# One stationary tile for the two parts of a small expert's tokens, and a branch around the third product

## Chip, core and metric

One core of a Trainium2 chip runs the whole program. Its engines work beside each other, each on its own list of instructions in order, and meet at semaphores: TensorE (PE, matrix products, with the weight loads PEld), VectorE (DVE), ScalarE (ACT), GpSimd (POOL) and SyncE (SP), which issues the loads from HBM. The metric is the device time of one execution in microseconds (us), the median of several.

## What is computed

The reference is two transformer blocks of two layers over 256 tokens of 1024 features, in float32. The change touches the last layer alone, a mixture of eight experts with 3584 hidden features each, of which every token takes two:

```python
D_MODEL, SEQ, N_EXPERTS, TOP_K, EXPERT_FF = 1024, 256, 8, 2, 3584

def swiglu_2(x, w_gate, w_up, w_down):
    return (jax.nn.silu(x @ w_gate) * (x @ w_up)) @ w_down

def moe_ffn(h, router_w, router_b, w_gate, w_up, w_down):
    t = h.reshape(b * s, d)
    logits = (t @ router_w).astype(jnp.float32) + router_b.astype(jnp.float32)
    top_vals, top_idx = lax.top_k(logits, TOP_K)
    top_w = jax.nn.softmax(top_vals, axis=-1)
    gates = jnp.sum(jax.nn.one_hot(top_idx, N_EXPERTS) * top_w[..., None], axis=1)
    for e in range(N_EXPERTS):
        y = swiglu_2(t, w_gate[e], w_up[e], w_down[e])
        out = out + gates[:, e:e + 1] * y
```

## The kernel before

Products keep float32's accuracy by splitting both operands into a rounded part and the rest, each in the format that TensorE takes at one column per cycle (float32r): x = xh + xl and w = wh + wl, and x w is xh wh + xl wh + xh wl. Three products stand for one. A weight arrives as a `raw` tile of 128 x 1024 (512 KB, one load on SP's queue, L320); ScalarE copies it to `hi` (L331, the rounded part) and VectorE subtracts to get `lo` (L332). There are 3 buffers for `hi`, 3 for `lo`, and in the experts 27 for `raw` once the pools of the layer before have been taken over.

`route` finds each token's two experts, its place (slot) at each of them and its gates. `gather` builds, for one expert or for a pair, one-hot matrices OH from the slots (tokens on partitions, 128 slots along), and multiplies the tokens' two parts HH and HL with them: XG holds an expert's tokens with features on partitions, 8 tiles of 128 x 128 for each part. It also makes OT (the one-hot transposed, to bring results back) and RX (the norm's scale of each slot).

The work of an expert goes in 7 steps `(e, fb)` of 512 hidden columns. `gate_up` makes two banks `gu` of 128 slots x 512 columns, gate and up: for each of 8 feature tiles k it takes XG's tile as the stationary operand and streams the weight,

```python
self.mm(ps, ps, xh, wh[:, c], k == 0, False)
self.mm(ps, ps, xl, wh[:, c], False, False)
self.mm(ps, ps, xh, wl[:, c], False, k == DT - 1)
```

48 products a step. Then come the activation `sl` (ScalarE's Silu, L1740; VectorE's product with up, L1741), and, one step later, `down`: four transposes of `sl` (L277), its two parts `hh` and `hl` (L357, L358), and 24 products into two banks `y`. After an expert's seventh step `scatter` brings `y` back to the tokens. Gathers are called after the fifth step of experts 0, 1, 3 and 5, for one, two, two and two experts; the first expert's stands ahead of all.

An expert may hold up to 128 tokens. If one has more, a second pass over all experts follows (`run(P)` under `tc.If(most > P)`, L1819); it is left out here. The order on each engine is set by a scheduler when the program is built: it may move instructions within a stretch of code without branches, and then it is fixed.

All matmuls are recorded by the helper `mm` (L259), so the profile's rows tell them apart by their tiles.

Of the kernel before, what the change touches and what calls it, by code (L numbers as in the profile page):

```python
# [9 lines left out]
F32 = mybir.dt.float32  # L10
F32R = mybir.dt.float32r
# [16 lines left out]
# ---------------------------------------------------------------- column layout of the packed vectors  # L28
# [35 lines left out]
def _const_arrays():  # L64
# [58 lines left out]
    # trailing means less the token itself: tokens s of a first tile to t of both, and of a second to its own  # L123
# [16 lines left out]
# ---------------------------------------------------------------- host layout  # L140
# [22 lines left out]
def _pack(inp):  # L163
# [9 lines left out]
    for l in range(2):  # L173
# [12 lines left out]
        # an even head's turned rows come after its others, an odd one's before  # L186
# [21 lines left out]
    # key and query, value, and gate tiles, in the order of the heads' work  # L208
# [34 lines left out]
# ---------------------------------------------------------------- kernel  # L243
class _K:
# [12 lines left out]
    # ---- tensor engine  # L257
# [21 lines left out]
    # ---- constants  # L279
# [27 lines left out]
    # ---- weights  # L307
# [45 lines left out]
    # ---- splits and norms  # L353
# [14 lines left out]
    def rows(self, cols, width, dst, tile_):  # L368
        """dst[f, t] = cols[t][:, head of f]: columns over tokens spread along the partitions."""
# [4 lines left out]
    def norm(self, acc, n, eps):  # L374
        """acc: [P, S] squares summed over feature tiles -> (columns [P, 2], rows [P, S])."""
# [25 lines left out]
    def prep(self, gname, gi):  # L401
        """Splits of x * g for all feature tiles, and the row scale to apply after the product."""
# [9 lines left out]
    # ---- dense feed forward  # L412
# [35 lines left out]
    # ---- rope tables  # L448
    def rope_tables(self, pool):
        nc = self.nc  # L450
        with self.tc.tile_pool(name="rope", bufs=1) as rp:
# [17 lines left out]
            for j in range(4):  # L469
                # phase of a quarter turn for the cosines  # L470
# [1467 lines left out]
```

## Time and profile before

| what | value |
|---|---|
| median of 3 runs | 2650.4 us (2649.74 to 2652.24) |
| span of the profiled execution | 2645.7 us |
| TensorE busy | 2605.0 us, 98% of the span |
| VectorE busy | 2001.3 us, 76% |
| ScalarE busy | 1610.3 us, 61% |
| loads of expert weights | 668 of 512 KB and 8 of 256 KB |
| mean granted TensorE clock | 0.995 |

The span runs from the first to the last instruction; the time of a run has some microseconds around it. The experts take about the last 1000 us. A share over the whole span mixes stages with different limits, so the views that matter are cut to the experts. The duration of a matmul overlaps the next one's, so what one costs is read from the distance between starts.

### The profile page before, as it was taken

What the parts mean: (1) busy time and instruction counts of PE and PEld (TensorE: products, weight loads), DVE (VectorE), ACT (ScalarE), POOL (GpSimd) and SP (SyncE); (2) the same over time, 40 slices, a digit from 0 to 9 for tenths busy, and PEclk for the clock granted to TensorE, in tenths of its full rate; (3) what the DMA queues carried; (4) which work ended last, traced back from release to release, by engine and by line L of the source; (5) the groups of instructions that cost most, each with busy time, mean ns of one, the idle gap of its engine ahead of it and who ended that gap; (6) DMA issues with size and microseconds to landing.
All of it is one profiled execution on the core that took longest, in us unless ns stands there. A gap on an engine that the chain in (4) does not pass through costs nothing.

```text
span 2645.7 us, 44986 instructions
## 1 busy us (share of the span) xinstructions
PE 2605.0 (98%) x17519; PEld 2365.1 (89%) x17519; DVE 2001.3 (76%) x2624; ACT 1610.3 (61%) x2208; POOL 86.7 (3%) x85
## 2 busy tenths in 40 slices
PE   8999999999999999999999999999999999999997
PEld 8999899999999899999999988888888888888886
DVE  7658567656658577656666867898989898989897
ACT  5444455444444555455445766777777777777776
POOL 0003000000003000000000200000000000000000
PEclk9999999999999999999999999999999999999999
DMA  6554125555554125555555339899999999999992
GB/s 232 190 183 160 56 79 163 187 184 184 185 184 159 62 81 172 187 185 167 188 187 166 120 132 338 312 336 355 336 367 354 341 351 364 352 340 354 363 353 96
DMA packets 166621, 602.08 MB, mean 228 GB/s; under 512 B 18704, under 2 KB 19232, under 8 KB 166400
## 3 DMA queue, kind: packets, MB, share of 16 engines
q1 hardware_dynamic: 165792, 596.92, 64.5%
q8 instruction: 139, 2.28, 0.3%
q0 software_dynamic: 608, 2.21, 0.3%
q14 instruction: 82, 0.67, 0.1%
HBM read 596.96 MB, written 1.05 MB: 226 GB/s over the span
## 4 chain that ended last, share of the span: by engine, by line
PE 93%; issue 3%; DVE 2%; ACT 1%; DMA 0%; POOL 0%; DVEq 0%; SPq 0%; ACTq 0%; POOLq 0%
PE m L259 24%; PE mm L259 23%; PE gu L259 22%; PE y L259 11%; PE s L259 6%; PE t L259 3%; PE x L259 1%; PE x L277 1%; PE s L500 1%; DVE lo L332 1%; PE u L259 1%; ACT hi L331 0%; PE c L259 0%; PE s L277 0%; ACT xh L360 0%
## 5 line engine op out<-in xcount | busy, mean ns | idle before, releaser
L331 ACT ACTIVATE hi<-raw 128x1024 fp32r<-128x1024 f32 x1128 | 1176.1, 1055 | 824.2 <-issue 323.3
L332 DVE TENSOR_TENSOR lo<-raw,hi 128x1024 fp32r<-128x1024 f32 x1128 | 1356.0, 1222 | 422.7 <-ACT hi L331 417.7
L259 PE MATMUL gu<-hi,XG 128*128 128x512 f32 x1792 | 559.9, 397 | 0.1
L259 PE MATMUL m<-xh,hi 128*128 128x256 f32 x1760 | 495.2, 281 | 9.2 <-ACT xh L360 8.7
L259 PE MATMUL m<-xh,lo 128*128 128x256 f32 x1760 | 495.4, 282 | 3.0 <-DVE lo L332 3.0
L259 PE MATMUL m<-xl,hi 128*128 128x256 f32 x1760 | 494.9, 281 | 1.8 <-DVE xl L361 1.8
L259 PEld LDWEIGHTS gu<-hi,XG 128*128 128x128 f32 x1792 | 337.1, 189 | 80.3 <-ACT hi L331 0.6
L259 PE MATMUL gu<-lo,XG 128*128 128x512 f32 x896 | 348.0, 398 | 0.0
L259 PEld LDWEIGHTS m<-xh,hi 128*128 128x128 f32 x1760 | 333.0, 189 | 9.8 <-ACT xh L360 9.1
L259 PEld LDWEIGHTS m<-xh,lo 128*128 128x128 f32 x1760 | 332.9, 189 | 3.9 <-DVE lo L332 3.9
L259 PEld LDWEIGHTS m<-xl,hi 128*128 128x128 f32 x1760 | 332.7, 189 | 2.4 <-DVE xl L361 2.4
L259 PE MATMUL mm<-hl,hi 128*128 128x256 f32 x880 | 248.2, 282 | 0.0
L259 PE MATMUL mm<-hh,lo 128*128 128x256 f32 x880 | 248.2, 282 | 0.0
L259 PE MATMUL mm<-hh,hi 128*128 128x256 f32 x880 | 247.6, 282 | 0.0
L259 PE MATMUL mm<-xh,hi 128*128 128x256 f32 x832 | 240.8, 290 | 6.1 <-DVE x L1128 3.2
L259 PE MATMUL mm<-xl,hi 128*128 128x256 f32 x832 | 239.9, 289 | 0.0
L259 PE MATMUL mm<-xh,lo 128*128 128x256 f32 x832 | 238.2, 287 | 0.1
L259 PEld LDWEIGHTS gu<-lo,XG 128*128 128x128 f32 x896 | 169.0, 189 | 41.4 <-DVE lo L332 0.9
L259 PE MATMUL y<-lo,hh 128*128 128x512 f32 x448 | 181.0, 404 | 0.0
L259 PE MATMUL y<-hi,hh 128*128 128x512 f32 x448 | 177.7, 397 | 0.7 <-ACT hh L357 0.7
L259 PE MATMUL y<-hi,hl 128*128 128x512 f32 x448 | 178.0, 397 | 0.0
L259 PEld LDWEIGHTS mm<-hl,hi 128*128 128x128 f32 x880 | 168.2, 191 | 0.0
(551 smaller groups left out, 3448.3 us busy)
## 6 DMA issues: line engine op xcount, KB each, us to landing
raw<-in_moe SPq DMA_DIRECT2D x668, 512.0 KB, 5.3
raw<-in_ffn SPq DMA_DIRECT2D x330, 512.0 KB, 4.2
raw<-in_win SPq DMA_DIRECT2D x56, 512.0 KB, 3.6
raw<-in_dnin SPq DMA_DIRECT2D x32, 512.0 KB, 3.5
raw<-in_wout SPq DMA_DIRECT2D x16, 512.0 KB, 3.5
raw<-in_pin SPq DMA_DIRECT2D x8, 512.0 KB, 4.3
raw<-in_dnout SPq DMA_DIRECT2D x8, 512.0 KB, 3.6
raw<-in_moe SPq DMA_DIRECT2D x8, 256.0 KB, 5.5
```

What stands on the lines that cost most here:

```text
L259: ins = self.nc.tensor.matmul(out, lhsT=lhsT, rhs=rhs, start=start, stop=stop)
L277: self.nc.tensor.transpose(out, in_, self.c("ident"))
L331: nc.scalar.activation(hi[:, c], raw[:, c], AF.Copy)
L332: nc.vector.tensor_tensor(lo[:, c], raw[:, c], hi[:, c].bitcast(F32), OP.subtract)
L500: nc.tensor.transpose(p4[:, h, :].bitcast(F32R), YP[:, h, 1, :], self.identr)
```

## The change

For an expert of at most 64 tokens (`few`), slots 64 to 127 are free. The rounded part of its tokens goes to slots 0 to 63 and the rest to slots 64 to 127 of the same stationary tile. With it, one product with wh gives xh wh in the upper half of the rows and xl wh in the lower, and the product with wl adds xh wl and xl wl. The third product is not needed. Since the Silu is not linear, gate's two halves have to be added before it: a matmul with the matrix FO (identity, plus the identity with its halves exchanged where the expert is small) folds the bank `gu[0]`, by way of a copy `both`. Up's halves need no fold, since everything behind them is linear and the scatter's one-hot now holds both slots of a token.

- `route`: the counts per expert are compared with 64.5, `few` and `many` are kept, `many` goes to the integer tile `ci` as well, and `keyl` is the slot for the rest (64 further on where the expert is small).
- `gather`: a second one-hot OL from `keyl`, OB as the maximum of both (in the room of `hh`) for OT and RX, and XG's first part as rounded part plus `few` times the rest, its second part times `many`.
- `gate_up`: the products with xl come last, in a branch that TensorE alone compares; the last product with wl stands behind it. All four `hi` of gate or of up are so held until then.
- `moe`: TensorE reads the eight `many` into registers before the first gather.
- buffers: `hi` has 3 + 4 (in turn), `raw` 21 where there were 27. The second pass (`base`) keeps its third product.

```diff
-NRB, NRC, NRD, NRE, NRF = 8, 12, 4, 3, 2
+NRB, NRC, NRD, NRF, NH2 = 8, 9, 4, 2, 4
...
-        hi = self.T(self.hip, [P, 1024], "hi", F32R)
+        self.nhi += 1
+        hi = self.T(self.hips[self.nhi % len(self.hips)], [P, 1024], "hi", F32R)
...
+        few, many = self.T(keep, [P, NE], "few"), self.T(keep, [P, NE], "many")
+        nc.vector.tensor_scalar(few, pc[:, 0:8], 64.5, None, OP.is_lt)
+        nc.vector.tensor_scalar(many, few, -1.0, 1.0, OP.mult, OP.add)
+        nc.vector.tensor_copy(ci[:, 1:], many)
+        keyl = self.T(keep, [P, 2, NE], "keyl")
+        nc.vector.scalar_tensor_tensor(keyl, few[:, None, :].broadcast_to([P, 2, NE]), 64.0, sel, OP.mult, OP.mult)
+        nc.vector.tensor_tensor(keyl, keyl, key, OP.add)
...
+                    nc.vector.tensor_scalar(OL[:, t, u, :], self.c("iota"), keyl[:, t, e:e + 1], None, OP.is_equal)
+
+            OB = self.T(p1, [P, 2, 2, P], "hh")[:, :, 0:w, :]
+            nc.vector.tensor_tensor(OB, OH.bitcast(F32), OL.bitcast(F32), OP.max)
...
-                if w == 2:
-                    nc.vector.tensor_copy(XG[0][:, :, k, :], p4[:, :, 0, :])
-                    nc.scalar.activation(XG[1][:, :, k, :], p4[:, :, 1, :], AF.Copy)
...
+                low = self.T(p1, [P, 2, P], "low")
+                nc.scalar.activation(low, p4[:, 1], AF.Copy)
+                for j in range(2):
+                    u, kk = (j, k) if w == 2 else (0, k + j)
+                    e = es[u]
+                    nc.vector.scalar_tensor_tensor(XG[u][:, 0, kk, :], low[:, j, :], few[:, e:e + 1], p4[:, 0, j, :],
+                                                   OP.mult, OP.add)
+                    nc.scalar.activation(XG[u][:, 1, kk, :], p4[:, 1, j, :], AF.Copy, scale=many[:, e:e + 1])
...
+            FO = self.T(pool, [P, 2, P], "FO")
+            if not base:
+                for u, e in enumerate(es):
+                    nc.vector.scalar_tensor_tensor(FO[:, u, :], SELF, few[:, e:e + 1], self.c("ident"), OP.mult, OP.add)
...
+                        for k in range(len(ws) - 2, len(ws)):
+                            self.mm(ps, ps, XG[:, 0, k, :], ws[k][0], k == 0, False)
+                            if k < DT - 1:
+                                self.mm(ps, ps, XG[:, 0, k, :], ws[k][1], False, False)
+
+                def third():
+                    for k in range(DT):
+                        self.mm(ps, ps, XG[:, 1, k, :], ws[k][0], False, False)
+
+                if base:
+                    third()
+                else:
+                    with tc.If(self.many[e] > 0):
+                        third()
+                self.mm(ps, ps, XG[:, 0, DT - 1, :], ws[-1][1], False, True)
...
+        def activate(gu, RX, FO):
+            if not base:
+
+                both = self.T(pool, [P, 512], "both")
+                nc.scalar.activation(both, gu[0], AF.Copy)
+                self.mm(gu[0], gu[0], FO, both, True, True)
...
+        pe = mybir.EngineType.PE
+        self.many = [nc.values_load(ci[0:1, 1 + e:2 + e], engines=(pe,), min_val=0, max_val=1) for e in range(NE)]
...
+            self.nhi, self.hips = -1, self.hips * 3 + [pool("hi2", NH2)] * NH2
```

The names in the order's rows are tiles: `gu` the two banks of a step, `hi` and `lo` the weight's parts, XG the gathered tokens, `x` a bank for gathers, transposes and scatters. TensorE, where gate of a step of the first expert ends and up begins, before:

```order
L259 MATMUL gu_20692<-hi_20721,XG_19699 128x512 x2
L259 MATMUL gu_20692<-lo_20722,XG_19699 128x512
L259 MATMUL gu_20692<-hi_20725,XG_19699 128x512 x2
L259 MATMUL gu_20741<-hi_20746,XG_19699 128x512 x2
L259 MATMUL gu_20692<-lo_20726,XG_19699 128x512
```

The same place in the changed kernel, where `gu_20286` is gate and `gu_20336` up:

```order
L259 MATMUL gu_20286<-hi_20315,XG_19795 128x512
L1772 COMPARE_AND_BRANCH
L259 MATMUL gu_20286<-hi_20291,XG_19795 128x512 x2
L259 MATMUL gu_20286<-hi_20295,XG_19795 128x512 x2
L259 MATMUL gu_20286<-hi_20311,XG_19795 128x512 x2
L259 MATMUL gu_20286<-hi_20315,XG_19795 128x512 x2
L1772 UNCONDITIONAL_BRANCH x2
L259 MATMUL gu_20286<-lo_20316,XG_19795 128x512
L259 MATMUL gu_20336<-lo_20342,XG_19795 128x512
```

The eight products with the second part moved behind all others but one, into the branch; each `hi` is read once ahead of it and twice within. Waits and semaphore instructions are left out of these rows.

TensorE at the start of the experts, between `route`'s last product and the first gather, before:

```order
L259 LDWEIGHTS onesb_19349
L259 MATMUL s_19625<-sel_19617,onesb_19349 128x8
L259 MATMUL x_19700<-OH_19696,HH_19344 128x128
L259 MATMUL x_19710<-OH_19696,HH_19344 128x128
L259 MATMUL x_19700<-OH_19696,HL_19345 128x128 x2
```

And in the changed kernel:

```order
L259 LDWEIGHTS onesb_19349
L259 MATMUL s_19625<-sel_19617,onesb_19349 128x8
L1858 TENSOR_LOAD ci_19651
L1858 ISA x2
L259 MATMUL x_19796<-OH_19787,HH_19344 128x128 x2
L259 MATMUL x_19796<-OL_19788,HL_19345 128x128 x2
```

Eight such reads of `ci` with their two register instructions each stand there now, one after another, ahead of the first gather.

TensorE at the end of a gather for one expert (its transposes and its product with RS), before:

```order
L259 MATMUL gu_20529<-lo_20539,XG_19699 128x512
L277 MATMUL x_20682<-c_id_82,OH_20638 128x128 x2
L259 MATMUL gu_20529<-hi_20558,XG_19699 128x512 x2
L259 MATMUL x_20687<-RS_19580,OH_20638 128x1 x2
L259 MATMUL gu_20529<-lo_20559,XG_19699 128x512
```

And in the changed kernel, where the one-hots' maximum lies in a tile `hh` and `sl` are the activations of two steps:

```order
L259 MATMUL gu_20917<-lo_20947,XG_19795 128x512
L259 MATMUL gu_21030<-hi_21035,XG_20788 128x512
L277 MATMUL x_20849<-c_id_82,hh_20786 128x128 x2
L259 MATMUL x_20854<-RS_19580,hh_20786 128x1 x2
L277 MATMUL x_20967<-c_id_82,sl_20864 128x128 x4
L277 MATMUL x_21130<-c_id_82,sl_21027 128x128 x4
L259 MATMUL y_3431_20058<-hi_20980,hh_20972 128x512
```

The transposes of two steps' activations now stand in a row behind the gather's, and the products `y` of the first of them follow at once.

## Rows read from the trace of the kernel before

**Rows 1.** Stretches: us, busy (x) PE, PEld, DVE, ACT, POOL; clock, DMA share, GB/s.

```profile
1650.00:2600.00 950.00, 950.00 (x4258) 768.38 (x4257) 852.46 (x827) 721.58 (x787) 0.00 (x0) 1.00 0.95 346
2062.16:2079.46 17.30, 17.30 (x77) 13.95 (x77) 15.35 (x15) 13.23 (x15) 0.00 (x0) 1.00 1.00 373
2200.00:2250.00 50.00, 50.00 (x221) 40.30 (x221) 44.57 (x41) 37.77 (x40) 0.00 (x0) 1.00 0.99 364
1595.00:1625.00 30.00, 27.14 (x219) 26.52 (x218) 20.67 (x54) 17.49 (x33) 0.71 (x1) 0.92 1.02 408
1620.00:1625.00 5.00, 5.00 (x23) 4.71 (x23) 1.89 (x7) 0.60 (x1) 0.00 (x0) 0.54 1.03 417
```

**Rows 2.** Waits from 1650 to 2600 us: total, times, longest, in us.

```profile
ACT hi L331 <- PE gu L259: 121.3, 221, 2.0
DVE lo L332 <- ACT hi L331: 92.5, 192, 1.4
...
DVE lo L332 <- DMA raw<-in_moe: 3.1, 7, 0.7
```

**Rows 3.** Chain of waits from 2000 to 2100 us: start, us, what.

```profile
2062.16 0.48 PE y L259 x2
...
2066.38 0.44 PE x L277 x4
...
2069.62 9.84 PE gu L259 x42
2079.46 0.47 PE y L259 x2
```

**Rows 4.** Groups of instructions, 1650 to 2600 us: count, busy us, mean ns, idle before.

```profile
L259 PE MATMUL gu<-hi,XG 128*128 128x512 f32 x1698 | 529.3, 397 | 0.0
L358 DVE TENSOR_TENSOR hl<-x,hh 128x512 fp32r<-128x512 f32 x53 | 36.2, 683 | 0.0
L357 ACT ACTIVATE hh<-x 128x512 fp32r<-128x512 f32 x53 | 30.8, 582 | 0.2
L1703 DVE CAST XG<-x 128x256 fp32r<-128x256 f32 x24 | 10.0, 418 | 0.8 <-PE x L259 0.6
L1691 DVE TENSOR_SCALAR OH<-c_dn,key 128x128 fp32r<-128x128 f32 x12 | 2.7, 278 | 0.0
```

**Rows 5.** Timeline of TensorE, a float32 product in the first block: start, us.

```profile
363.45 2.86 PE L259 MATMUL t<-Uc,raw 128*128 128x256 f32 x12
365.95 0.82 PE L259 MATMUL s<-wE,SK 128*128 128x256 f32 x4
```

**Rows 6.** Timeline of TensorE near the end, a product behind a wait.

```profile
2632.73 0.50 PE L259 MATMUL x<-yh,OT 128*128 128x512 f32 x1 [0.15 <-DVE ACC L1781]
2633.06 0.40 PE L259 MATMUL x<-yl,OT 128*128 128x512 f32 x1
```

**Rows 7.** The branch over the second pass: ns min/median/max, first and last start.

```profile
L1819 PEldq COMPARE_BRANCH  x1: 3355/3355/3355, 2634.0 to 2634.0; - x1
L1819 POOLq COMPARE_BRANCH  x1: 45/45/45, 2636.7 to 2636.7; - x1
L1819 POOLq EVENT_SEMAPHORE  x1: 17/17/17, 2636.9 to 2636.9; - x1
L1819 PEldq EVENT_SEMAPHORE  x1: 51/51/51, 2637.4 to 2637.4; - x1
L1819 DVEq COMPARE_BRANCH  x1: 72/72/72, 2637.6 to 2637.6; - x1
```

**Rows 8.** SP's read of one count, and the first gather's start.

```profile
L1811 SPq TENSOR_LOAD <-ci x1: 476/476/476, 1619.5 to 1619.5; - x1
L1811 SPq SEQ_ASSERT  x1: 33/33/33, 1620.3 to 1620.3; - x1
1619.24 0.52 PE L259 MATMUL x<-OH,HH 128*128 128x128 f32 x3 [0.65 <-DVE OH L1691]
```

**Rows 9.** Waits of SP's queue from 1650 to 2600 us: total, times, longest, in us.

```profile
SPq L320 <- DVE lo L332: 664.3, 609, 7.4
```

More of the change, by code (lines that the diff above doesn't have):

```diff
@@ L1662, in route, with experts @@
         nc.vector.tensor_reduce(cm, pc[:, 0:8], AX.X, OP.max)
-        ci = self.T(keep, [P, 1], "ci", I32)
-        nc.vector.tensor_copy(ci, cm)
-        return HH, HL, ACC, RS, GT, key, ci
-    def experts(self, base, HH, HL, ACC, RS, GT, key, st):
+        ci = self.T(keep, [P, 1 + NE], "ci", I32)
+        nc.vector.tensor_copy(ci[:, 0:1], cm)
+        few, many = self.T(keep, [P, NE], "few"), self.T(keep, [P, NE], "many")
[5 more added lines that the diff above has]
+        nc.vector.tensor_tensor(keyl, keyl, key, OP.add)
+        SELF = self.T(keep, [P, P], "SELF")
+        nc.vector.tensor_copy(SELF[:, 0:64], self.c("ident")[:, 64:128])
+        nc.vector.tensor_copy(SELF[:, 64:128], self.c("ident")[:, 0:64])
+        return HH, HL, ACC, RS, GT, (key, keyl, few, many, SELF), ci
+    def experts(self, base, HH, HL, ACC, RS, GT, keys, st):
         nc, tc = self.nc, self.tc
+        key, keyl, few, many, SELF = keys
         def open_(name, bufs):
@@ L1683, in experts @@
             nc.vector.tensor_scalar(kb, key, float(base), None, OP.subtract)
-            key = kb
+            key = keyl = kb
         def gather(es):
             w = len(es)
-            OH = self.T(p1, [P, 2, 2, P], "OH", F32R)[:, :, 0:w, :]
+            OH, OL = [self.T(p1, [P, 2, 2, P], n, F32R)[:, :, 0:w, :] for n in ("OH", "OL")]
             for t in range(2):
@@ L1718, in gather @@
                 for t in range(2):
-                    self.mm(ps, ps[:, u:u + 1], OH[:, t, u, :].bitcast(F32), RS[:, t:t + 1], t == 0, t == 1)
+                    self.mm(ps, ps[:, u:u + 1], OB[:, t, u, :], RS[:, t:t + 1], t == 0, t == 1)
             RX = self.T(pool, [P, 2], "RX")
             nc.vector.tensor_copy(RX[:, 0:w], ps[:, 0:w])
-            return [(XG[u], OT[:, u], RX[:, u:u + 1]) for u in range(w)]
+            FO = self.T(pool, [P, 2, P], "FO")
+            if not base:
+                for u, e in enumerate(es):
+                    nc.vector.scalar_tensor_tensor(FO[:, u, :], SELF, few[:, e:e + 1], self.c("ident"), OP.mult, OP.add)
+            return [(XG[u], OT[:, u], RX[:, u:u + 1], FO[:, u, :]) for u in range(w)]
         def gate_up(e, fb, XG, RX):
@@ L1795, in experts @@
                     late.append(open_("moey", 1))
-                sl = gate_up(e, fb, G[e][0], G[e][2])
+                gu = gate_up(e, fb, G[e][0], G[e][2])
             if pend is not None:
@@ L1805, in experts @@
                     G += gather([pe + 1, pe + 2])
-            cur = G[e] if e is not None else None
-            pend = (e, fb, sl, cur) if e is not None else None
+            if e is not None:
+                pend = e, fb, activate(gu, *G[e][2:4]), G[e]
     def moe(self, HH, HL, ACC, RS, GT, key, ci):
@@ L1855, in build @@
             self.nraw, self.rawp, self.once, self.ahead = -1, [ring], [], []
-            self.hip = pool("hi", 3, side="right")
+            self.nhi, self.hips = -1, [pool("hi", 3, side="right")]
             self.lop = pool("lo", 3, side="right")
@@ L1913, in build @@
                 stx.close()
[L1914 to L1916 removed]
+            self.nhi, self.hips = -1, self.hips * 3 + [pool("hi2", NH2)] * NH2
+            self.nraw, self.rawp = -1, [ringb] * NRB + [ringc] * NRC + [ring] * 4
+            self.once, self.ahead = rest + [ring] * 4, ahead
             self.psx = pool("psx", 2, space=PSUM)
```

31 lines of the change are left out of this document (12 added, 19 removed).

## The prediction, as it was put on record

> **What bounds the kernel now.** I read the busy time by stretch first [rows 1]. The eight experts run from about 1620 to 2632 us. From 1650 to 2600 us TensorE is busy for all 950 us at a granted clock of 1.00, VectorE for 852 us, ScalarE for 722 us, and the DMA engines have a share of 0.95. The waits of that stretch say who follows whom [rows 2]: no matmul stands in the list, ScalarE's `hi` waits for TensorE to free a buffer (121.3 us behind `gu` alone), VectorE's `lo` for `hi` (92.5 us), and either for a weight's DMA only 3.1 us. The chain of waits is then TensorE alone [rows 3]: 42 gate and up products in 9.84 us, 0.2343 us each, and from 2062.16 to 2079.46 one step (one block of 512 hidden columns of one expert): 17.30 us. Counted out, 72 products x 0.2343 + 0.44 us for the four transposes = 17.31 us. So TensorE waits for nothing, and a product left out there is worth 0.234 us until another engine is late. That other engine is close: the same step holds 15.35 us of VectorE [rows 1].
>
> The stretch has 1698 gate and up products with `hi` [rows 4], 32 to a step, so 53.1 steps: 17.90 us each for TensorE (0.6 us of it gather and scatter), 852.46 / 53.1 = 16.05 us for VectorE, 13.6 us for ScalarE. There are 56 steps.
>
> **How often the product goes.** The reference's router, worked out on its own default inputs, gives the experts 64, 59, 68, 59, 84, 64, 57 and 57 tokens. So six have at most 64 (42 steps) and two have more (14 steps).
>
> **TensorE, an expert of few tokens.** Gone: 16 products x 0.2343 = 3.75 us. New: the fold, a 128x512 product of two plain float32 operands. No such row exists; the nearest is 128x256 in float32, which the profile shows as two instructions, 12 of them from 363.45 to 365.95 us [rows 5]: 0.208 us each, 0.417 us for 256 columns, 0.83 for 512. I take 0.85. New too: two skipped branches. In the built program the skipped side is a wait until TensorE's own count stands at everything issued so far, a jump, and on. So the queue runs empty each time. The matmul ends 0.397 us after its start, where the next would have started at 0.234: 0.16 us. After a wait the first product takes 0.50 us, and the next starts 0.33 us after it [rows 6]: 0.10 us more. An event instruction of TensorE took 51 ns and a compare 45 to 72 ns on four engines [rows 7]; with the jump some 0.15 us. Sum 0.41; I take 0.45 us a skip. The ends are far apart: not below 0.16 us, which the drain alone takes [rows 4, 6], and up to 3.36 us, which TensorE's one compare took where it left out the whole second pass of the experts [rows 7]. I take the low end because this jump passes 8 products and their weight loads, not thousands of instructions; POOL, whose skipped part is one instruction, went on 0.2 us after its compare.
>
> The Trainium skill (Runtime: NRT & Kernel Launch, Instruction fetch mechanics) says that a taken branch whose target lies outside the part of the program held at the engine waits for a fetch. By that rule the 3.36 us are such a fetch, which agrees with the row, and it speaks against this change: a skip pays it where its target lies past the end of what is held, and what that would make of the time stands with the rivals.
>
> Step: 17.90 - 3.75 + 0.85 + 0.90 = 15.9 us.
>
> **VectorE takes over.** Its 16.05 us stay and the gather grows, per pair of experts: four more one-hot fills (0.278 us), one maximum over 128x512 (nearest 0.683 us), two masks (0.28), and 16 three-operand writes of 128x128 for eight casts of 128x256 at 0.418 us [rows 4]; a new one lies between the 0.278 of that shape and the 0.418, I take 0.3. Sum 1.1 + 0.7 + 0.6 + 1.5 = 3.9 us per pair, 0.28 us per step: 16.3 us. So with 15.9 for TensorE and 16.3 for VectorE the step is VectorE's. It never ran at 100%, since it waits for `hi`, and `hi` for buffers that TensorE frees. The change raises `hi` from three buffers to seven but holds four until the branch. I walked a step through by hand: after a gate's branch the next four `hi` are made in 4 us while three `lo` (3.5 us) are still to be made from `hi` that exist, so VectorE has work. I add 0.3 us for what does not fit: 16.6 us.
>
> ScalarE gains the copy `both` (0.58 us, as `hh`) and 0.34 us of gather: 14.5 of 16.6 us, hidden. DMA: 12 loads of 512 KB in 16.6 us are 379 GB/s against 364 in the best 50 us of this stretch and 408 with a deep queue [rows 1]: it just fits, with 21 buffers where there were 27. Each other engine also gets a jump per branch, 112 of them at some 0.05 us, beside operations of 1.2 us: hidden; bare, 6 us.
>
> **An expert of many tokens** keeps every product and stays TensorE's: 17.90 + 0.85 + 2 x 0.1 for compare and jump = 18.95 us.
>
> **The start.** TensorE now reads eight counts before the first gather. On SP such a read took from 1619.5 to 1620.3 us with what belongs to it [rows 8], 0.85 us; eight are 6.8 us, on the path, since the gather began at 1619.24 us [rows 8], as soon as its one-hot was there. I take 7. After the wait for the router the granted clock was 0.54 for 5 us [rows 1], near the lower of its two levels; a longer wait meets the same fall, so I add nothing for it.
>
> **Gathers.** The new maximum tile takes the room of `hh`, so the next step's `hh` waits for its readers: the order shows two steps' transposes in a row behind them. `hh` and `hl` then stand bare (0.58 + 0.68 us): 1.3 us x 4 gathers, 5 us.
>
> **Sum.** 42 x (16.6 - 17.9) = -55; 14 x (18.95 - 17.9) = +15; start +7; gathers +5: -28 us. The profiled execution spans 2645.7 us against a median of 2650.4, 4.7 us lie around it, and the change is the same in both: 2618 in the span, **2622 us**.
>
> **Rivals.** *The skip is dear.* TensorE's step is 15.0 + 2s us with a skip of s. At s = 1.2 it is 17.4, 42 x 0.5 = 21 us of gain, and the 27 us of cost eat it: from there the kernel is slower. At 2 us the step is 19.0: +46 + 27, 2723 us; at the 3.36 us of the row it is 21.7 and the time 2837; if one skip in ten pays that, 8 x 3.36 = 27 us more, 2649, no change. For it: the one compare that TensorE ran. Against: its distance, and that four engines' compares took 0.07 us or less. The Trainium skill's rule on fetches (above) would make it some of the skips, not all. *DMA is the next bound.* At 364 GB/s, the best 50 us [rows 1], a step takes 6.29 MB / 364 = 17.3 us: -25 + 27, 2652 us, no change. For it: a share of 0.99 there; against it: 0.95 in the mean, 408 GB/s with a deep queue, and SP's waits, which are for VectorE to free a buffer, 664 us [rows 9]. *The two engines fit without loss* and skips hide: 15.9 us, -84 + 27, 2593 us. *The change doesn't do what it says:* if the two experts at exactly 64 count as many, 28 x -1.3 + 28 x 1.05 + 12 = +5, 2655 us.
>
> **How the numbers follow.** 0.2% is 5 us, about what a measurement of this kernel can tell. Forecast with its own range of 2605 to 2640 us: 0.57, all faster. Dear skips, all or some: 0.20, of it 0.16 slower, 0.04 the same. DMA: 0.13, split 0.04 faster, 0.05 same, 0.04 slower. No loss: 0.06. Not as it says: 0.04, half same, half slower. Faster 0.67, same 0.11, slower 0.22. The range goes down to 2596 (part of the no-loss case stays out) and up to 2690, a skip of 1.6 us; some 0.16 of the chance lies outside.
>
> **What would show it.** Waits of TensorE for `lo` in the experts of few tokens, VectorE above 95% busy there, steps of 16.6 us in experts 0, 1, 3, 5, 6, 7 and near 19 us in 2 and 4; gaps of 0.45 us in TensorE before the last `lo` product of gate and of up; the first gather some 7 us later. It is wrong if the gaps are over 1 us, if `lo` or `hi` wait for DMA, or if VectorE is idle while TensorE waits, which would mean that the held `hi` buffers starve it.

## Result: 70 us slower

The changed kernel takes 2720.4 us (median of 4 runs, 2720.2 to 2721.6) where the kernel before took 2650.1 us beside it (4 runs, 2649.0 to 2652.2): a ratio of 1.027, with a 95% interval of 1.0255 to 1.0284. The forecast was 2622 us in a range of 2596 to 2690: wrong in its sign and outside its range. The profiled execution spans 2718.3 us, 72.6 more than before.

From the profile page of the changed kernel: busy time, share of the span and instructions of each engine.

```profile
PE 2581.9 (95%) x16959; PEld 2265.3 (83%) x16959; DVE 2011.6 (74%) x2696; ACT 1628.6 (60%) x2332; POOL 87.3 (3%) x85
```

Its busy times by stretch, with the columns of [rows 1]: the experts, a stretch in which the tokens of experts 2 and 3 are gathered, and one step of a small expert.

```profile
1650.00:2680.00 1030.00, 943.34 (x3796) 684.86 (x3795) 871.37 (x892) 749.81 (x912) 0.00 (x0) 0.97 0.89 325
...
1882.00:1902.00 20.00, 11.49 (x42) 8.58 (x40) 8.87 (x27) 11.22 (x24) 0.00 (x0) 0.63 0.32 127
2096.79:2113.79 17.00, 15.61 (x64) 10.95 (x63) 15.15 (x15) 13.14 (x16) 0.00 (x0) 1.00 0.98 361
```

Before, TensorE was busy for every microsecond of the experts [rows 1]. Now it is busy for 943 of 1030 us, VectorE for 871, the DMA share has fallen from 0.95 to 0.89: no engine is full, so they wait for each other. In the 20 us of the gather no engine is busy for 60%, and the granted clock there is 0.63.

The waits of the changed kernel from 1650 to 2680 us (total, times, longest) answer to [rows 2]:

```profile
ACT hi L332 <- issue: 93.1, 47, 3.1
...
DVE lo L333 <- PE gu L259: 54.9, 49, 2.4
ACT hi L332 <- PEq L1772: 53.8, 25, 2.7
PEld y L259 <- ACT hi L332: 42.4, 57, 1.1
...
PEld gu L259 <- ACT hi L332: 31.9, 40, 3.0
```

ScalarE's `hi` now waits for L1772, the branch (53.8 us by name; of the 93.1 us put down to "issue", for which the view names no releaser, 58.7 us end within 0.4 us of a skip's last instruction). And TensorE's weight loads now wait for `hi`, which is not in the list before. It is a circle.

To see where the time went, take the distances between the starts of VectorE's `sl` (L1741 before, L1786 after): there is one in each of the 56 steps, so 55 distances, the time ahead of the first and the time behind the last. The distances fall into 12 in which a gather runs (the last three of experts 0, 1, 3 and 5), 14 that start in the experts of many tokens, 2 and 4, and 29 others of small experts. Worked out so from each profiled execution, less the same of the kernel before (1639.8 us ahead of the first, 504.3 in the 29 steps, 227.1 in the 12, 245.9 in the 14, 28.7 behind the last; it took 2648.7 to 2650.1 us beside these runs):

| kernel | median us | ratio to before (95%) | start | 29 small steps | 12 gather steps | 14 large steps |
|---|---|---|---|---|---|---|
| after | 2720.4 | 1.0270 (1.0255 to 1.0284) | +13.0 | -1.9 | +43.0 | +18.4 |
| e1_no_branch | 2639.2 | 0.9956 (0.9942 to 0.997) | +10.3 | -39.7 | +15.3 | +6.6 |
| e2_hold_one | 2652.7 | 1.0012 (1.0002 to 1.0022) | +14.8 | -34.2 | +19.7 | +7.7 |
| e3_hi_11 | 2682.7 | 1.0122 (1.0106 to 1.0139) | +19.9 | -21.8 | +26.0 | +11.6 |
| e4_rooms | 2690.6 | 1.0154 (1.0137 to 1.0171) | +15.7 | -7.9 | +22.0 | +13.2 |
| e5_gather_sum | 2676.6 | 1.0103 (1.0086 to 1.0119) | +11.0 | -8.6 | +7.0 | +18.7 |
| e6_no_branch_gather_sum | 2610.4 | 0.9851 (0.9835 to 0.9867) | +3.3 | -33.9 | -12.4 | +6.5 |
| e7_hold_two | 2697.3 | 1.0181 (1.0164 to 1.0198) | +14.3 | -13.8 | +33.9 | +15.0 |
| e8_hold_two_gather_sum | 2669.1 | 1.0075 (1.0056 to 1.0093) | +10.6 | -12.7 | +10.1 | +12.0 |
| e9_no_branch_gather_sum_hh2 | 2606.4 | 0.984 (0.9824 to 0.9857) | +6.5 | -39.2 | -12.3 | +4.4 |
| e10_hold_two_gather_sum_hh2 | 2662.9 | 1.0052 (1.0035 to 1.0069) | +16.8 | -14.7 | +8.5 | +11.8 |
| e11_hi_10_gather_sum_hh2 | 2655.5 | 1.0025 (1.0014 to 1.0036) | +11.9 | -16.8 | -1.1 | +14.5 |
| e12_both_on_vector | 2671.1 | 1.0081 (1.0064 to 1.0098) | +18.0 | -11.9 | +11.5 | +10.2 |
| e13_up_only_hi_7 | 2640.8 | 0.9973 (0.9963 to 0.9982) | +6.2 | -11.4 | -7.1 | +5.8 |
| e14_up_only_hi_9 | 2636.8 | 0.9954 (0.9937 to 0.997) | +9.3 | -14.7 | -9.6 | +8.3 |

The four columns are of one execution each; the one of e10 took 5 us more than e10's median.

By the prediction's own sum the row of the changed kernel should have read +7, 29 x -1.3 = -38, 12 x -1.3 + 5 = -11, +15. So the start missed by 6 us, the large experts by 3, the small steps by 36 and the gathers by 54: together 99 us, for the 98 between 2622 and 2720. The two big ones are the question.

The 36 us of the small steps don't lie evenly. The first two distances of experts 1, 3, 5 and 6, behind the end of the expert before, take 17.0 and 23.8 us, where they took 19.7 and 16.8: 17 us more for the eight, where 10 less had been forecast. The other 21, of 17.0 us mostly, take 19 us less, where 27 had been forecast.

### The profile page after: what moved, and what is told of

Same layout as the page of the kernel before. It is cut to its first block, busy times and chain, and to the rows that moved or that the text cites. A ratio compares the mean times of both kernels' runs of the same rounds, so it can differ in the third digit from the quotient of the medians.

```text
span 2718.3 us, 44878 instructions
## 1 busy us (share of the span) xinstructions
PE 2581.9 (95%) x16959; PEld 2265.3 (83%) x16959; DVE 2011.6 (74%) x2696; ACT 1628.6 (60%) x2332; POOL 87.3 (3%) x85
## 5 line engine op out<-in xcount | busy, mean ns | idle before, releaser
L332 ACT ACTIVATE hi<-raw 128x1024 fp32r<-128x1024 f32 x1128 | 1142.3, 1052 | 823.5 <-issue 420.6
L259 PE MATMUL gu<-hi,XG 128*128 128x512 f32 x1120 | 404.7, 400 | 18.5 <-ACT hi L332 16.6
L259 PE MATMUL gu<-lo,XG 128*128 128x512 f32 x896 | 381.9, 433 | 19.5 <-DVE lo L333 6.1
L259 PEld LDWEIGHTS gu<-hi,XG 128*128 128x128 f32 x1120 | 211.2, 189 | 88.0 <-ACT hi L332 33.8
L259 PE MATMUL y<-hi,hh 128*128 128x512 f32 x448 | 188.4, 425 | 29.9 <-ACT hi L332 17.2
L259 PE MATMUL y<-lo,hh 128*128 128x512 f32 x448 | 173.7, 401 | 0.0
L259 PEld LDWEIGHTS mm<-hh,lo 128*128 128x128 f32 x880 | 168.3, 191 | 0.0
```

The source lines that it names most:

```text
L259: ins = self.nc.tensor.matmul(out, lhsT=lhsT, rhs=rhs, start=start, stop=stop)
L332: nc.scalar.activation(hi[:, c], raw[:, c], AF.Copy)
```

## A small step: held `hi`

ScalarE and VectorE in the step of 17.00 us shown above: start, us, instruction, and in brackets the idle time before it with what ended it.

```profile
2101.40 0.58 ACT L358 ACTIVATE hh<-x 128x512 fp32r<-128x512 f32 x1
2103.15 3.91 ACT L332 ACTIVATE hi<-raw 128x1024 fp32r<-128x1024 f32 x4 [1.18 <-issue]
2106.97 0.57 ACT L1782 ACTIVATE both<-gu 128x512 f32<-128x512 f32 x1
2110.22 2.96 ACT L332 ACTIVATE hi<-raw 128x1024 fp32r<-128x1024 f32 x3 [2.68 <-PEq L1772]
...
2103.73 4.62 DVE L333 TENSOR_TENSOR lo<-raw,hi 128x1024 fp32r<-128x1024 f32 x4
2108.63 1.23 DVE L333 TENSOR_TENSOR lo<-raw,hi 128x1024 fp32r<-128x1024 f32 x1 [0.28 <-issue]
2110.81 2.36 DVE L333 TENSOR_TENSOR lo<-raw,hi 128x1024 fp32r<-128x1024 f32 x2 [0.95 <-PE gu L259]
2113.79 0.75 DVE L1786 SCALAR_TENSOR_TENSOR sl<-gu,RX,sl 128x512 f32<-128x512 f32 x1 [0.62 <-ACT sl L1785]
```

TensorE's waits for `hi` in the same step:

```profile
2105.22 0.50 PE L259 MATMUL y<-hi,hh 128*128 128x512 f32 x1 [0.69 <-ACT hi L332]
...
2107.12 0.50 PE L259 MATMUL y<-hi,hh 128*128 128x512 f32 x1 [0.23 <-ACT hi L332]
```

ScalarE stops for 2.68 us until the branch behind up has freed the bank's first `hi`, and 1.18 us earlier on. Each stop ends just behind a branch. TensorE then waits for the `hi` made behind gate's branch (0.69 and 0.23 us), and so comes later to up's. VectorE idles for 0.28 + 0.95 + 0.62 us: with its 15.15 us of work that makes the 17.00. The first two of these waits are not for `hi`: they end with TensorE's products with `lo`, the 0.95 us with the product behind up's branch, which frees a buffer of `lo`. The third is for ScalarE's `sl`, which stands behind the `hi` that came late. So all three engines turn on TensorE's way to the branch. The skip itself is no matter. TensorE's last product ahead of that branch and the first behind it, from the timeline:

```profile
2109.70 0.40 PE L259 MATMUL gu<-hi,XG 128*128 128x512 f32 x1
2110.24 0.47 PE L259 MATMUL gu<-lo,XG 128*128 128x512 f32 x1
```

The branch's own instructions, from the view of L1772: count, then least, median and most ns, first and last start:

```profile
L1772 PEldq COMPARE_BRANCH  x140: 65/202/368, 1641.0 to 2688.0; - x140
L1772 PEldq EVENT_SEMAPHORE  x84: 51/51/51, 1642.4 to 2688.8; - x84
```

The 84 skips are 42 steps x 2, as predicted. From the last product ahead of a skip to the first behind it are 0.54 us, 0.31 more than between two products, and in all 84 places between 0.30 and 0.32. The Trainium skill's rule (Runtime: NRT & Kernel Launch, Instruction fetch mechanics) that a taken branch whose target lies outside what the engine holds waits for a fetch shows in none of them.

A step of the other kind, behind the end of expert 2 (2072.99 to 2096.79 us), has 40 `y` products in it where the step above has 24, since a part of the step before's falls into it. ScalarE's stops for the branches stand in it too, this one and one of 2.73 us:

```profile
2086.10 3.90 ACT L332 ACTIVATE hi<-raw 128x1024 fp32r<-128x1024 f32 x4 [2.23 <-PEq L1772]
```

**e1, the branch away.** Small experts make no third product, large ones make it in its old place; no reads of counts.

```diff
+                            if base or e in (2, 4):
+                                self.mm(ps, ps, XG[:, 1, k, :], ws[k][0], False, False)
...
-                    with tc.If(self.many[e] > 0):
-                        third()
...
-        self.many = [nc.values_load(ci[0:1, 1 + e:2 + e], engines=(pe,), min_val=0, max_val=1) for e in range(NE)]
```

> The changed kernel without its branches and without the eight register reads: which experts are small is written into the program for this input (0, 1, 3, 5, 6, 7 make no third product; 2 and 4 make it in its old place, beside each weight's first product). The packed tokens, the fold, the longer gather, 7 buffers for hi and 21 for raw stay as in the change. Changed kernel 2720 us, before 2650. Theory A (the branches cost: hi held until the branch, and work that can't be ordered across a branch): a step of a small expert is VectorE's 16.3 to 16.6 us instead of 17.0, the steps behind an expert's end lose their 4.3 us, gathers spread among the products again; worked out as in the prediction without skips and reads, 42 x (16.45 - 17.9) + 14 x 0.85 + 10 us for start and gathers = -39 us against before, 2611 us, 2600 to 2635. Rival B (fold, gather and VectorE cost, branches don't): start 6 of the 13 us and the gathers' 43 us stay, so 2690 to 2710 us.

2639.2 us: 81 us below the changed kernel, so theory A holds in size, though its 2600 to 2635 was too hopeful: the small steps came down by all that had been forecast (-39.7), the gathers only from +43 to +15. The eight distances behind an expert's end keep 4 of their 17 us with no branch at all; what holds those is open.

**e2, the branch stays and holds one.** It tells the two halves of theory A apart.

```diff
                             self.mm(ps, ps, XG[:, 0, k, :], ws[k][0], k == 0, False)
+                            if base or (e in (2, 4) and k < DT - 2):
+                                self.mm(ps, ps, XG[:, 1, k, :], ws[k][0], False, False)
...
-                    for k in range(DT):
+                    for k in range(DT - 2, DT):
                         self.mm(ps, ps, XG[:, 1, k, :], ws[k][0], False, False)
```

> The branches stay at their places, in all experts, but hold only the last two of the eight third products, which read the last hi; in experts 2 and 4 the other six stand in their old place (written into the program for this input), in the small ones they are left out as in the change. So the branch, its skip and the cut in the program's order stay, and of the four held hi one is. If the held buffers are what starves the engines (theory A1): clean steps of small experts go from 17.0 to about 16.4 us, some 30 x 0.6 = 18 us, and the 4.3 us at each of six experts' ends and a part of the gathers' 43 us go: 2660 to 2690 us. If it is the cut in the order and the skip (theory A2): within 6 us of the changed kernel, 2714 to 2726 us.

2652.7 us, below what A1 gave and far from A2: with the branches, skips and reads all in place, holding one `hi` in place of four is worth 68 us. Of the 66 between the two profiled executions 32 lie in the small steps (12 of them in the eight behind an expert's end), 23 in the gather steps, and 11 in the large experts, whose products e2 also moves back to their old place. Branches, skips and reads together are the rest to e1, 13 us. One step of a small expert without the branch (e1), by stretch:

```profile
1806.47:1821.47 15.00, 14.79 (x63) 10.92 (x63) 15.00 (x16) 13.36 (x16) 0.00 (x0) 1.00 1.03 409
```

And one with a branch that holds one (e2):

```profile
2448.80:2464.20 15.40, 15.03 (x62) 10.65 (x61) 14.99 (x15) 13.49 (x16) 0.00 (x0) 1.00 1.02 401
```

Without the hold VectorE is full and the step is 15.0 us. The 16.3 us that the prediction took for VectorE's work were the mean of all steps; one without gather and scatter had 15.35 us of it before the change [rows 1].

**e3, more buffers** in place of fewer held.

```diff
-NRB, NRC, NRD, NRF, NH2 = 8, 9, 4, 2, 4
+NRB, NRC, NRD, NRF, NH2 = 8, 5, 4, 2, 8
```

> The changed kernel with 11 buffers for hi in place of 7, and 17 for raw in place of 21 to make room. Theory A1 (held hi): with four held there are 7 left to run ahead in, as good as without a hold: 2660 to 2690 us, unless loads come late with 17 buffers, which would show as waits of hi or lo for a DMA above 20 us in the experts. Theory A2 (cut order, skip): 2714 to 2726 us. Theory B (rooms of the gather): 2714 to 2726 us.

2682.7 us: as A1 says, 38 us less, with no wait for a DMA among the long ones. But the small steps gain 20 us of the 32 that e2 gains: 14.4 to 16.8 us each. ScalarE's longest wait in total is now another, `hh` for the `y` products of the step before (70.0 us from 1660 to 2620 us).

**e7, two held**, by twice as many branches; nothing left out.

```diff
-                def third():
-                    for k in range(DT):
-                        self.mm(ps, ps, XG[:, 1, k, :], ws[k][0], False, False)
+                    def third():
+                        for k in range(4 * q, 4 * q + 4):
+                            self.mm(ps, ps, XG[:, 1, k, :], ws[k][0], False, False)
```

> The changed kernel with a branch after each pair of hi, four to a step in place of two, so that two hi are held in place of four; nothing is left out. With one held (e2) a clean step was 15.2 to 15.4 us, with four 17.0. Held buffers: TensorE's own step is 72 - 16 products, the fold and four skips, 13.1 + 0.44 + 0.85 + 4 x 0.35 = 15.8 us, VectorE's 15.0; clean steps of 15.8 to 16.2 us, 2660 to 2685 us. If a branch costs by itself more than a held buffer does: above 17.0 us a step, 2720 us or more.

2697.3 us, a gain of 23 us and 12 us short of what was expected: steps of 15.7 to 16.8 us. Twice the branches are not dearer than the two buffers that they free, but they give little.

## The gather: a chain through two engines

TensorE, ScalarE and VectorE of the changed kernel while the tokens of experts 2 and 3 are gathered:

```profile
1888.15 0.80 PE L259 MATMUL x<-OH,HH 128*128 128x256 f32 x2 [3.01 <-ACT XG L1732]
...
1889.99 0.80 PE L259 MATMUL x<-OH,HH 128*128 128x256 f32 x2 [0.62 <-ACT XG L1732]
...
1887.99 0.38 ACT L1726 ACTIVATE low<-x 128x256 f32<-128x256 f32 x1
1888.78 0.37 ACT L1732 ACTIVATE XG<-x,many 128x128 fp32r<-128x128 f32 x1 [0.42 <-DVE XG L1730]
1889.57 0.37 ACT L1732 ACTIVATE XG<-x,many 128x128 fp32r<-128x128 f32 x1 [0.42 <-DVE XG L1730]
1889.83 0.38 ACT L1726 ACTIVATE low<-x 128x256 f32<-128x256 f32 x1
...
1900.75 0.60 ACT L358 ACTIVATE hh<-x 128x512 fp32r<-128x512 f32 x1 [2.65 <-PE x L277]
1904.36 1.06 ACT L332 ACTIVATE hi<-raw 128x1024 fp32r<-128x1024 f32 x1 [3.02 <-PE y L259]
...
1888.40 0.35 DVE L1730 SCALAR_TENSOR_TENSOR XG<-low,few,x 128x128 fp32r<-128x128 f32 x1 [0.71 <-ACT low L1726]
1889.18 0.35 DVE L1730 SCALAR_TENSOR_TENSOR XG<-low,few,x 128x128 fp32r<-128x128 f32 x1 [0.43 <-ACT XG L1732]
```

Each new operation takes what the prediction gave it (0.35 us for 0.3). But they follow each other: `low` on ScalarE, XG on VectorE, XG on ScalarE, both once more, then TensorE's next bank, 1.84 us from one `low` to the next. Of the eight rounds of this gather the last five (`low` from 1887.99 to 1895.93 us) have no `hi` and no `lo` between them: while they run, the weights stand still, TensorE with them. Behind them ScalarE waits for the transposes of two steps and for `y` products, and makes the next `hi` at 1904.36 us. In the gather for experts 4 and 5 the last four rounds stand so, in that for 6 and 7 the last two; the three distances of these gathers take 72.7, 69.3 and 65.3 us, where each took 57.0. Fewer such rounds cost less, but the last gather loses 8 us with two. Before the change a bank had two casts, with `hi` and `lo` and products of gate and up between:

```profile
2096.50 0.42 DVE L1703 CAST XG<-x 128x256 fp32r<-128x256 f32 x1
2096.75 0.37 ACT L1704 ACTIVATE XG<-x 128x256 fp32r<-128x256 f32 x1
2097.08 1.06 ACT L331 ACTIVATE hi<-raw 128x1024 fp32r<-128x1024 f32 x1
```

**e4, rooms of its own** for the maximum OB, and two buffers for `low`.

```diff
-            OB = self.T(p1, [P, 2, 2, P], "hh")[:, :, 0:w, :]
+            OB = self.T(p1, [P, 2, 2, P], "OB")[:, :, 0:w, :]
...
-                low = self.T(p1, [P, 2, P], "low")
+                low = self.T(pool, [P, 2, P], "low")
```

> The changed kernel with a room of its own for the maximum OB (it shared hh's) and two buffers for low; 20 buffers for raw in place of 21. If the gathers' 43 us and the late start come from these rooms (theory G): the steps with a gather lose 8 to 10 us each and the start 2 us, 2675 to 2690 us. If they come from the branch, behind which a gather's work is not ordered among other products (A2), or from held hi (A1): each gather 1 to 2 us better, 2712 to 2720 us.

2690.6 us, 30 us less, near theory G: the gathers give 21 of it back, not the 32 to 40 expected, and the start nothing. The run changes both rooms at once. Its gathers for a pair take 70.2, 65.2 and 54.5 us: the last, made of the same operations, is below the 57.0 of before. There `hi` stand between them on ScalarE:

```profile
2405.95 0.38 ACT L1726 ACTIVATE low<-x 128x256 f32<-128x256 f32 x1
2406.23 1.05 ACT L332 ACTIVATE hi<-raw 128x1024 fp32r<-128x1024 f32 x1
2407.18 0.36 ACT L1732 ACTIVATE XG<-x,many 128x128 fp32r<-128x128 f32 x1
2407.43 1.06 ACT L332 ACTIVATE hi<-raw 128x1024 fp32r<-128x1024 f32 x1
```

As far as this gather shows, the rounds cost what the order of the program makes of them; the three operations more that a bank has cost little there.

**e5, another gather.** TensorE adds the two parts, so that the copies are those of before. The maximum with its room in `hh` goes as well.

```diff
+                        nc.vector.tensor_scalar(OL[:, t, u, :], self.c("iota"), keyl[:, t, e:e + 1], few[:, e:e + 1],
+                                                OP.is_equal, OP.mult)
...
+                    for i, parts in enumerate((((HH, OH), (HL, OL)) if not base else ((HH, OH),), ((HL, OH),))):
+                        for n, (src, one) in enumerate(parts):
+                            for t in range(2):
+                                self.mm(ps, p4[:, i, j * w:j * w + w, :], src[:, t, (k + j) * P:(k + j) * P + P], one[:, t],
+                                        n == 0 and t == 0, n == len(parts) - 1 and t == 1)
+                if w == 2:
+                    nc.vector.tensor_copy(XG[0][:, :, k, :], p4[:, :, 0, :])
+                    nc.scalar.activation(XG[1][:, :, k, :], p4[:, :, 1, :], AF.Copy)
```

> The changed kernel with another gather: TensorE adds the two parts itself (products of HH with OH and of HL with OL into one bank, OL filled as one-hot times few, so that it is empty for a large expert), XG is written by one 128x256 copy for each expert as before the change, and OT and RX come from OH and OL in turn, so that OB, its room and low are gone. Branches and the four held hi stay. If the gathers' 43 us come from the chain that ScalarE and VectorE take in turn (low 0.38, XG 0.35, XG 0.37, XG 0.35, XG 0.37 us, 1.85 us a feature tile where TensorE has 0.8 us of products): 3 x 12 + 4 = 40 us less, 2675 to 2690 us. If they come from the branch, behind which a gather's work can't be ordered among other products: 2710 to 2720 us.

2676.6 us: 44 us less, 36 of it in the gather steps, though the branches are all there. TensorE at the gather of experts 2 and 3 in e5, where the gather's products stand among others again:

```profile
1858.32 0.40 PE L259 MATMUL x<-OH,HH 128*128 128x256 f32 x2
...
1858.80 0.39 PE L259 MATMUL x<-OH,HL 128*128 128x256 f32 x2
1859.03 0.40 PE L259 MATMUL gu<-lo,XG 128*128 128x512 f32 x1
```

So it was this gather's own form, chain and rooms together, and not that work can't be ordered across a branch. How the 36 us divide between the two isn't shown: e4 leaves the chain in and gives 21.

**e6, e5's gather without the branch.**

> e1_no_branch (which experts are small is written into the program for this input) with the gather of e5. e1 gave 2639 us, its clean steps 15.0 us, its steps with a pair's gather 28.6 to 32.8 us. If those steps' extra 14 to 18 us are the chain of copies: 3 x 13 = 39 us less, 2595 to 2610 us. If they are something else (the order of TensorE's work around a gather): 2630 to 2640 us.

2610.4 us, 29 us below e1: the gather alone again, chain and rooms, the held buffers being out of the way. This and e9 are what the packing is worth on this input when nothing is decided at run time: 1.5 to 1.6%.

## Looking for a version that decides at run time

**e8**, e7 and e5 together.

> e7 and e5 together; nothing is left out and nothing is written into the program for this input. If held buffers and the gather's chain are the two causes and apart from each other, the gains add: e7's time less 35 to 40 us, about 2630 us (2615 to 2650), below the kernel before. If the gather's loss goes away with the held buffers, e7's time less 10 us or so, 2660 us.

2669.1 us: 28 us below e7 where 35 to 40 were expected, and still above the kernel before. The two causes add up only in part; the small steps stay at 16.1 to 16.8 us. ScalarE's longest wait, from 1660 to 2600 us, is then this one (total, times, longest):

```profile
ACT hh L358 <- PE y L259: 72.4, 25, 4.2
```

**e9, e10, e11: two buffers for `hh` and `hl`**, in e6, in e8, and in e5 with 10 for `hi`.

```diff
-            hh = self.T(p1, [P, 4, P], "hh", F32R)
-            hl = self.T(p1, [P, 4, P], "hl", F32R)
+            hh = self.T(pool, [P, 4, P], "hh", F32R)
+            hl = self.T(pool, [P, 4, P], "hl", F32R)
```

> e6 (no branch, which experts are small written into the program for this input; TensorE sums the gather) with two buffers for hh and hl in place of one, 20 for raw. In e6 the clean steps of experts 1 and 3 took 15.0 us, those of 5 to 7 16.2 us, with ScalarE's hh waiting for the y products of the step before. If that wait is the one buffer of hh: 15.0 us there too, some 14 x 1.2 = 17 us less, about 2593 us. If it is the order that the program was given there: 2605 to 2613 us.

2606.4 us, 4 us below e6 and not 17, in the range given for the other reading, the program's order: the late steps came down from 16.2 to 15.5 us, and a gather step took part of it.

> e8 (branch after each pair of hi, so two held; TensorE sums the gather; nothing left out) with two buffers for hh and hl, 20 for raw. e8's clean steps in the later experts took 16.8 us, with TensorE busy for 15.7; ScalarE waited 2.6 us in each for the y products that read hh. If hh's buffer sets the 16.8 us: 15.8 to 16.1 us, some 25 x 0.8 + 5 = 25 us less, 2640 to 2650 us. If the branches do: 2664 to 2674 us.

2662.9 us, 6 us below e8: the late steps are at the expected 16.1 us, but those of the first two experts rose to 17.9.

> The change's own two branches a step and four held hi, with 10 buffers for hi, two for hh and hl, 17 for raw and TensorE's sum in the gather; nothing left out. e3 (11 for hi) had clean steps of 16.4, later 16.8 us with hh waiting. If buffers are what the held hi take and the rest is hh: clean steps of 15.4 to 15.8 us, 2630 to 2645 us, below the kernel before. If the hold costs whatever the buffers (work behind it can't be ordered ahead): 16.4 us and 2655 to 2670 us.

2655.5 us, 7 us above the kernel before: with buffers enough, four held cost less than two held with twice the branches, and both end at steps of 16.1 us where e9 has 15.0 to 15.5.

**e12, the copy `both` on VectorE.** In e11 ScalarE waits 49.2 us for gate's bank (2200 to 2580 us) with `hi` copies queued behind.

```diff
-                nc.scalar.activation(both, gu[0], AF.Copy)
+                nc.vector.tensor_copy(both, gu[0])
```

> e11 with the fold's copy both made by VectorE in place of ScalarE. If the copy's place in ScalarE's queue sets the 16.1 us (hi copies stand behind its wait for gate): VectorE's step is 15.0 + 0.6 = 15.6 us, some 30 x 0.5 = 15 us less than e11's 2655 us, 2638 to 2645 us. If the branch does: 2655 us or, as VectorE has more to do, up to 2665 us.

2671.1 us, 16 us slower than e11, with late steps of 16.3 us: the place of `both` alone doesn't set the 16.1 us. VectorE has more to do than ScalarE (15.3 and 12.2 us of a late step), and the wait for gate only moved to the next in ScalarE's list, `sl` (47.8 us in the same stretch). So a wait for gate in that list, with `hi` behind it, isn't ruled out as the cause.

**e13 and e14, only up packed**, so no fold and one branch a step; 7 and 9 buffers for `hi`.

```diff
+                            g = 2 if m and not base else 0
+                            self.mm(ps, ps, XG[:, g, k, :], ws[k][0], k == 0, False)
+                            if not m:
+                                self.mm(ps, ps, XG[:, 1, k, :], ws[k][0], False, False)
...
+                if m:
+                    if base:
+                        third()
+                    else:
+                        with tc.If(self.many[e] > 0):
+                            third()
```

> Only up is packed: gate's stationary tiles hold the rounded part in both halves of the slots and the rest in both halves, and gate makes all three products in their old place; up's tile holds the rounded part in slots 0 to 63 and the rest in 64 to 127, and up's third product stays in a branch. So there is no fold, no both, one branch a step, and hi is held in up alone. 7 buffers for hi, two for hh and hl, 18 for raw. TensorE's step is 64 x 0.2343 + 0.44 + 0.35 = 15.8 us, VectorE's 15.0. If the fold and gate's hold were the rest of the loss: steps of 15.8 to 16.1 us, 42 x (15.95 - 17.3) + 14 x 0.2 + 15 us for start and gathers = -39, about 2611 us (2600 to 2625), below the kernel before. If one held bank costs as much as two: steps of 16.8 us and 2640 us or more.

2640.8 us, faster than both kernels (0.27% under the one before), but 16 us above the top of what was expected, and where the other reading, that one held bank costs as much as two, had put it: steps of 16.2 us in the first experts, 17.0 from the fourth on.

> e13 with 9 buffers for hi and 16 for raw. If up's four held hi still starve ScalarE and VectorE with 7 buffers: 10 to 20 us less than e13. If they don't: within 5 us of e13, and above it by more if 16 buffers for raw are too few.

2636.8 us, 4 us less than e13: buffers were no longer the matter. This version beats the kernel before by 0.46% (0.30 to 0.63) and the changed one by 3.1% (2636.8 to 2720.4 us), with counts read at run time. An early and a late step of it, by stretch:

```profile
1814.83:1830.02 15.19, 15.04 (x68) 11.94 (x66) 15.09 (x16) 12.73 (x15) 0.00 (x0) 1.00 1.03 407
2456.07:2473.12 17.05, 16.14 (x69) 12.18 (x68) 15.06 (x14) 12.66 (x15) 0.00 (x0) 1.00 1.00 379
```

ScalarE in the late one, from the timeline:

```profile
2458.85 5.80 ACT L332 ACTIVATE hi<-raw 128x1024 fp32r<-128x1024 f32 x6
2467.65 0.69 ACT L1778 ACTIVATE sl<-gu,RX 128x512 f32<-128x512 f32 x1 [3.00 <-PE gu L259]
2468.24 5.79 ACT L332 ACTIVATE hi<-raw 128x1024 fp32r<-128x1024 f32 x6
```

And VectorE behind it:

```profile
2469.32 3.50 DVE L333 TENSOR_TENSOR lo<-raw,hi 128x1024 fp32r<-128x1024 f32 x3 [1.68 <-ACT hi L332]
```

VectorE has 15.1 us of work in either. In the late one ScalarE comes to `sl` 3.00 us before its bank is done, with six `hi` behind, and VectorE waits 1.68 us for the first of them. That the place of `sl` in the fixed list makes the two us is argued from these rows; no run moved it, and it stays open.

## Why the prediction was wrong, step by step

- **What bounds the kernel now**: TensorE, with VectorE close behind. Right, but VectorE's size was wrong. The 16.05 us are a mean that holds gather and scatter, some 0.6 us a step (32.9 us of `XG`, `OH` and `ACC` by the groups from 1650 to 2600 us, over 53.1 steps), and the 15.35 us of a step without them [rows 1] are the busy time of an engine that waits before most instructions. Where it doesn't wait, the next starts before the one ahead has ended: eight `lo` in a row in the changed kernel take 9.18 us, 1.148 each, where one alone takes 1.22. A full step is then 15.0 us (e1). This error hid a part of the next one.

```profile
1643.61 9.18 DVE L333 TENSOR_TENSOR lo<-raw,hi 128x1024 fp32r<-128x1024 f32 x8 [2.60 <-ACT hi L332]
```

  The Trainium skill (Perfetto Trace Analysis, DVE / Act Engine Instruction) says that the reported time runs to the acknowledged write, while the next instruction may begin its prefetch before that; these rows agree.
- **Six experts of few tokens, 84 skips**: right. **Products**: right. **Fold**: 0.85 predicted; from 2108.61 to 2109.70 us the fold and one product take 1.09, so 0.86. **Skip**: 0.45 predicted, 0.31 measured. The dear skip, the rival that held most of the slower side, was wrong: the kernel is slower for another reason.
- **"I walked a step through by hand ... so VectorE has work. I add 0.3 us"** is the step that failed, for the small steps: 17.0 us for 16.6, and for a possible 15.2 to 15.4 (e2). The walk looked at the time behind gate's branch, and there VectorE does have work: four `lo` from 2103.73 us on. It left out the time ahead of each: with four of seven held and three made ahead, ScalarE must stop until TensorE comes to the branch, and TensorE itself waits on its way for `hi` that ScalarE could make only behind the branch before. VectorE is busy for 89% of such a step, not for the 95% that the prediction wanted to see. e2 put the small steps at -34 us against before, where the prediction said -38. The prediction took one mean for all steps, too: 28 of the 36 us lie in the eight behind an expert's end, and e2 and e1 leave these 5.5 and 4.4 us above before. The prediction named this case, "the held `hi` buffers starve it", as what would make it wrong, and gave it neither a price nor a chance.
- **Gathers, 5 us**, is the larger miss, 54 us. The operations were counted one by one and set beside other work (3.9 us of VectorE a pair, hidden or spread over the steps). What they cost is set by their order: a chain through three engines, whose last two to five rounds of a pair's eight stand in a row with the weights' work outside them, and behind it two steps' transposes and `y` products. Rooms of their own for the maximum and `low` give back 21 us with the chain left in (e4), rooms and chain away together 36 (e5); the share of each is not shown.
- **Start, +7**: measured +13. The eight reads do take 0.72 us each, from 1621.2 to 1627.0 us. But most of that lies beside a wait that the prediction didn't see: with more buffers ScalarE makes four `hi` ahead of the Exp for the gates, and VectorE's one-hots stand behind what waits for it.

```profile
1618.64 3.92 ACT L332 ACTIVATE hi<-raw 128x1024 fp32r<-128x1024 f32 x4
1622.59 1.28 ACT L1652 ACT_TABLE_LOAD   x1
...
1624.12 0.17 DVE L1654 TENSOR_SCALAR w<-w 128x2 f32<-128x2 f32 x1 [2.61 <-ACT w L1652]
...
1625.13 0.29 DVE L1705 TENSOR_SCALAR OH<-c_dn,key 128x128 fp32r<-128x128 f32 x1
...
1627.27 0.66 PE L259 MATMUL x<-OH,HH 128*128 128x128 f32 x2 [7.17 <-DVE hh L1709]
```

  Without the reads (e1) the start is still +10.3 us. With e5's gather, which has no maximum to wait for, it is +11.0 us with reads and branches and +3.3 without (e6): there most of the 7 us shows. The sum was near for a wrong reason.
- **Many tokens, +15**: measured +18.4, right but for 3 us.
- **DMA as the next bound**: no. e1's step of 15.0 us runs at 409 GB/s with 21 buffers, and waits for loads are not among its long ones.
- **The clock** was taken as 1.00. In the gather's 20 us it was 0.63, and 0.50, the lower of its two levels (1.2 GHz), while the chain ran and TensorE waited for `XG`:

```profile
1888.00:1904.00 16.00, 12.12 (x42) 9.79 (x43) 5.82 (x20) 6.21 (x18) 0.00 (x0) 0.50 0.02 9
```

  The products behind it follow each other at 0.43 us, not 0.23 (from 1902.84 to 1904.12 us), until it rises again at 1904.4. That adds to the gather: the mean granted clock is 0.981 in the changed kernel, 0.992 in e5.

## What to carry to other kernels

When a change makes a buffer live longer, count how many stay free while it is held, and follow the engine that fills them up to the moment of release, not only from it. Walk the odd steps as well as the plain one: here the eight behind an expert's end held most of the small steps' miss. When operations are added between two engines, write down who waits for whom, multiply the length of one round by the rounds, and look in the program's order for what stands between them, before asking whether the engines have room. And the busy time of an engine that waits overstates what it needs: price it where it runs without a gap.

## What the runs showed of the hardware

A skipped branch of eight products and their weight loads on TensorE costs 0.31 us, each of 84 times, wait for its own count and jump included; its compare has ended before the last product ahead of it starts, each time. VectorE's `lo` costs 1.148 us in a row and 1.22 alone. Products of 512 columns follow each other at 0.43 us at a granted clock of 0.50 and at 0.234 at 1.00. The loads keep up 409 GB/s over a whole step (e1), above the 364 of the best 50 us of [rows 1].
